# Load buffers moved to multiples of 512 bytes, two more of them, 4096-byte rows for the experts' second layers, and an earlier place for the overflow branch

## The chip, the cores and the metric

The kernel runs on one core of a Trainium2 chip. The metric is the device time of one execution in microseconds (us); lower is better. The kernel before has a median of 1852.47 us in 3 runs (1851.46 to 1853.66).

## What is computed

Two transformer blocks on 256 tokens of width 1024, all in float32. The first block has a mixer (sparse attention and block attention) and a mixture of 32 experts, of which each token uses 4. The second block puts 16 meta tokens ahead (272 rows) and has a stick-breaking attention layer, an MLP, a gated linear recurrence, a second MLP and a last norm. The part that the change is mostly about is the mixture of experts:

```python
def sparse_moe(h, router_w, router_b, w1, b1, w2, b2):
    logits = (hf @ router_w + router_b).astype(jnp.float32)
    top_val, top_idx = lax.top_k(logits, TOP_K)              # 4 of 32
    gate = jax.nn.softmax(top_val, axis=-1)
    ...
    def expert_block(args):
        e, toks, wts = args
        u = hf[toks] @ w1[e] + b1[e]                          # 1024 -> 2048
        g_, lin = u[:, :D_FF], u[:, D_FF:]
        g_ = jnp.minimum(g_, SWIGLU_LIMIT)
        lin = jnp.clip(lin, -SWIGLU_LIMIT, SWIGLU_LIMIT)
        y = ((lin + 1.0) * g_ * jax.nn.sigmoid(SWIGLU_ALPHA * g_)) @ w2[e] + b2[e]   # 1024 -> 1024
        return y * wts[:, None]
    y = lax.map(expert_block, ...)
    return jax.ops.segment_sum(...)
```

`exp_w1` is 32 x 1024 x 2048 and `exp_w2` 32 x 1024 x 1024 float32, 402.7 MB in all, or 384 transfers of 1 MB (1,048,576 bytes). Every weight is read once.

## The kernel before

**Loads.** The class `Stream` holds a list of load items of up to 1 MB in the order of use. `pump` issues them from the SP queue (L169) into `wraw` tiles of 128 partitions x 2048 floats. A load is issued when the buffer that comes next in the rotation is free. The rotation has a fixed depth, and `widen(places, until)` adds buffers in named places of an arena (`r1`, `s2`, ...) up to an item number. Each DMA counts on one of eight semaphores (`DMAHW0` to `DMAHW7`), which are used in turn, and a load waits until the one before it on its semaphore has landed, so at most eight are in flight. In the dense layers `split_to` turns each raw tile into a high and a low part (ACT copies at L189, DVE or POOL subtracts at L191); the experts use the raw tiles.

**Experts.** The 32 experts are sorted by their number of tokens and worked off in 17 jobs: 15 pairs with 64 slots each and two single ones with 128. `queue_moe` queues w1 of job i (8 items for each expert, 128 rows of 8192 bytes), then w2 of job i-1 (4 items for each expert). The 16 w1 items of the first job are known before the routing (`known`); all later ones are addressed by the routing result. A w2 item is 256 rows of 1024 floats, laid out so that partition p has rows 2p and 2p+1, one run of 8192 bytes. `moe` runs, for i from 0 to 17, `mm1` of job i (PE, L1442, and the bias, L1444), then its activation `act_steps` (DVE L1468, L1465, L1472, L1475 and ACT L1469 on the tile `gl`, which sits in arena place s5, and the transposes `turn`, PE L1501 and ACT L1502, and `slots`), then `mm2` of job i-1 (PE L1535, evictions on ACT L1543 and DVE L1544, and the sum back into the tokens, PE L1558 and L1559, DVE L1563). The `turn` steps of job i are run between the matmuls of `mm2` of job i-1. The last items are therefore w1 of the last job (353 to 368), w2 of the last but one (369 to 376) and w2 of the last (377 to 384).

**Gather.** Ahead of each group of jobs `gather` picks the tokens' rows with a 0/1 matrix `S`: four fp32r matmuls for a tile of 128 rows (L1407: two token halves x a high part `h2h` and a low part `h2l`), and one DVE instruction (L1409).

**Overfull experts.** An expert with more tokens than its slots leaves the rest to `overflow`: all engines read a count (L1230) and branch on it (`tc.If`, L1231); the body loops over the experts. With this input the count is zero and the body is jumped over. The body's first two loads for each expert go into the tile `ovb`, in arena place s5. `moe` calls it at i = n = 17, after the last activation steps are queued and before `mm2` of the last job:

```python
                    first, second = self.act_steps(self.jobs[i], ctxs[i])
                    self.bg += first
...
                if i >= 1:
                    if i == n:
                        self.overflow()
                        self.st.cut = "DP"
                    out = self.mm2(self.jobs[i - 1], ctxs.pop(i - 1))
```

**Norms of the second block.** `norm_in` squares and adds eight tiles; in its part 1 POOL squares the even ones (L1638), ACT the odd ones (L1640), and POOL and DVE add (L1647), beside DVE's `hn_lo` (L1628).

Of the kernel before, what the change touches and what calls it, by code (L numbers as in the profile page):

```python
# [20 lines left out]
S = 256  # L21
# [196 lines left out]
def _v(pattern, **kw):  # L218
    return lambda t: t.rearrange(pattern, **kw)
# [23 lines left out]
class Ker:  # L243
# [86 lines left out]
    def setup(self):  # L330
        nc, A = self.nc, self.A
        cp = self.cp = self.pool("const")
        self.cst = cp.tile([128, A["keep"].shape[1]], F32, name="cst")
        self.h = cp.tile([128, 8, NT], F32, name="h")
        self.tmp = self.pool("tmp", 2)
        self.eps = cp.tile([128, 1], F32, name="eps")
        nc.vector.memset(self.eps, EPS)
        nc.scalar.preload_act_table_set(LNEXP)

        def c(name):  # L340
            o, n = self.koff[name]
# [17 lines left out]
    def queue_pre(self):  # L359
# [47 lines left out]
        for c in range(2):  # L407
            cs = slice(c * 512, c * 512 + 512)
            st.add([(lambda t, b=b: t.rearrange("p (k n) -> p k n", k=4)[64 * b:64 * b + 64],
                     wo[256 * b:256 * b + 256, cs].rearrange("(k p) n -> p k n", p=64)) for b in range(2)],  # L410
                   [lambda t, m=m: t.rearrange("p (k n) -> p k n", k=4)[:, :, m * 256:m * 256 + 256] for m in range(2)])
            more(2)
        for c in range(2):
            add_half(st, wo[:, c * 512:c * 512 + 512], 512, 512)
# [81 lines left out]
    def pre(self):  # L496
# [4 lines left out]
        with ExitStack() as ctx:  # L501
# [13 lines left out]
            self.queue_moe()  # L515
            self.queue_post()
            self.widen(("r1", "r2", "r3"), self.early)

# [20 lines left out]
            for k in range(8):  # L539
                self.square_in(k, h[:, k, X], S)  # L540
            self.acc = self.ar("s4", [128, 2, 256], F32, "acc")
            s1, s0 = self.ada(1, pa, "tp"), self.ada(0, self.ps_m, "ot")
# [38 lines left out]
    def mixer(self, H, L):  # L581
# [9 lines left out]
        zs = [self.ar("r0", [128, 8, S], F32, "z")]  # L591
        alibi = self.ar("s6", [128, 8, 384], BF16, "alibi")
        gh = pp.tile([128, 8, 24], F32R, name="gh")
# [69 lines left out]
        kcbd = pp.tile([128, 32], F32, name="kcbd")  # L663
        kr = pp.tile([128, 4, 32], F32, name="kr")
        hd = pp.tile([128, 4, 32], F32, name="hd")

# [58 lines left out]
        for i in range(6):  # L725
            self.dense_t(0, H, L, S, ev_norm(0, i, 6), 2 * (i // 3))
            if i == 1:
                self.st.ahead = 4
        self.fill(len(self.bg))
        heads_rs(0)  # L730

        vv = self.vvt[:, 0:1536].rearrange("p (c n) -> p c n", c=2)
# [171 lines left out]
        for i in range(2):  # L904
            self.dense_v(H, L, lambda c, ps, i=i: nc.scalar.copy(out=vm[:, c, i * 256:i * 256 + 256], in_=ps))
        while state.get("done", -1) < 3:
            self.fill()
# [84 lines left out]
    def route_tile(self, m):  # L992
# [3 lines left out]
        if m == 0:  # L996

            self.ms = self.pp.tile([128, 2, 4], F32, name="ms")
            self.xn = self.ar("s2", [128, 2, 1024], F32, "xn")
# [29 lines left out]
    def route(self):  # L1029
# [19 lines left out]

        self.h2h = self.ar("s3", [128, 2, 1024], F32R, "h2h")  # L1050
        self.h2l = self.ar("s4", [128, 2, 1024], F32R, "h2l")
        xn = self.xn

        def rows(q, c, e):
            o = slice(q * 512, q * 512 + 512)
            r, hi, lo, x = rn[:, 0, c:c + 1], self.h2h[:, c, o], self.h2l[:, c, o], self.nat[c][q]
            if e is nc.scalar:
                e.activation(out=hi, in_=x, func=AF.Copy, scale=r)
            elif e is nc.vector:
                e.scalar_tensor_tensor(out=lo, in0=x, scalar=r, in1=hi.bitcast(F32), op0=ALU.mult, op1=ALU.subtract)  # L1060
            else:
                nc.scalar.activation(out=xn[:, c, o], in_=x, func=AF.Copy, scale=r)
                e.tensor_tensor(out=lo, in0=xn[:, c, o], in1=hi.bitcast(F32), op=ALU.subtract)

        for q in range(2):
            for c in range(2):
                rows(q, c, nc.scalar)

# [10 lines left out]
        for c in range(2):  # L1079
            nc.vector.tensor_scalar(out=sel[:, c], in0=lg[:, c], scalar1=mx[:, c, 3:4], scalar2=None, op0=ALU.is_ge)  # L1080
        rows(0, 0, nc.vector)
        for c in range(2):
            rows(1, c, nc.gpsimd)

# [16 lines left out]
        pick()  # L1101
        rows(0, 1, nc.vector)
        for _ in range(3):
# [47 lines left out]
    def gates(self, pool):  # L1151
# [5 lines left out]
        nc.vector.tensor_tensor(out=g, in0=self.g4, in1=r.unsqueeze(2).to_broadcast([128, 2, 4]), op=ALU.mult)  # L1157
        eg = pool.tile([128, 8, 32], F32, name="geq")
        nc.vector.tensor_tensor(out=eg, in0=self.eq, in1=g.rearrange("p c j -> p (c j)").unsqueeze(2).to_broadcast([128, 8, 32]),
# [65 lines left out]
    def overflow(self):  # L1225
# [5 lines left out]
        with tc.If(n > 0):  # L1231
            ep, pm = self.ep, self.pm

            h2 = self.ar("s2", [128, 8, S], F32, "h2")
            xr = self.ar("s1", [128, 2, 1024], F32, "ovr")
            nc.vector.tensor_tensor(out=xr, in0=self.h2h.bitcast(F32), in1=self.h2l.bitcast(F32), op=ALU.add)
            for k in range(8):
# [9 lines left out]
            with tc.For_i(0, N_EXP, 1) as e:  # L1247
# [4 lines left out]
                nc.sync.dma_start(out=bb, in_=A["exp_b1"][0, bass.ds(e, 1), :].rearrange("a (m p) -> p (a m)", p=128))  # L1252
                act = self.ar("s6", [128, 8, S], F32, "ova")
                for m in range(8):
# [36 lines left out]
    def queue_moe(self):  # L1291
# [26 lines left out]
        def add_w2(ps):  # L1318
            for k in range(4):
                for p in ps:  # L1320

                    st.add([(lambda t: t, lambda p=p, k=k: A["exp_w2"][0, expert(p), k * 256:k * 256 + 256, :]
                             .rearrange("a (p k) n -> p (a k n)", k=2))], ["raw"])

# [9 lines left out]
    def moe(self):  # L1334
        nc, tc = self.nc, self.tc
        with ExitStack() as ctx:
# [10 lines left out]
            for i in range(n + 1):  # L1347
                if i < n:
# [29 lines left out]
    def gather(self, gi):  # L1378
# [8 lines left out]
        if gi:  # L1387
            sel = self.ep.tile([128, 2, 256], F32R, name="S", tag="S")
        else:
            sel = self.ar("sg", [128, 2, 128], F32R, "S0")  # L1390
        xs = self.xs[gi] = self.ar(f"s{1 + gi % 2}", [128, 8, 256], F32, "xs")
# [9 lines left out]
        def tile(k):  # L1401
            def go():
                g = self.gather_bank()[:, 0:tot]
                ks = slice(k * 128, k * 128 + 128)
                for i, x in enumerate((self.h2h, self.h2l)):
                    for c in range(2):
                        nc.tensor.matmul(g, lhsT=x[:, c, ks], rhs=sel[:, c, 0:tot], start=(i == c == 0), stop=(i == c == 1))  # L1407

# [43 lines left out]
    def act_steps(self, job, c):  # L1452
# [40 lines left out]
        def turn(q):  # L1493
            def go():
# [4 lines left out]
                for k in range(4):  # L1499
                    kk = q * 4 + k  # L1500
                    nc.tensor.transpose(t[:, k * 128:k * 128 + 128], l.rearrange("s (q p k) -> s q k p", p=128, k=2)[:, kk // 2, kk % 2], self.c("ident"))  # L1501
                nc.scalar.copy(out=c["at"][:, q * 4:q * 4 + 4], in_=t.rearrange("p (k s) -> p k s", k=4))  # L1502
# [107 lines left out]
    def norm_in(self, name, j, n, by_token=False):  # L1610
# [10 lines left out]
        def norm(k, src, part=None):  # L1621
# [13 lines left out]
            else:  # L1635
                sq = self.pc.tile([128, NT], F32, name="sq", tag="nsq", bufs=2)[:, :n]
            if part == 1 and k % 2 == 0:
                nc.gpsimd.tensor_tensor(out=sq, in0=src, in1=src, op=ALU.mult)  # L1638
            else:
                nc.scalar.activation(out=sq, in_=src, func=AF.Square)  # L1640
            if part == 1:

                if k < 2:
                    sums.append(sq)
                else:
                    e = nc.vector if k % 2 else nc.gpsimd
                    e.tensor_tensor(out=sums[k % 2], in0=sums[k % 2], in1=sq, op=ALU.add)  # L1647
                acc = sums[0]
# [612 lines left out]
```

## Time and profile before

| what | value |
|---|---|
| median of 3 runs | 1852.47 us (1851.46 to 1853.66) |
| profiled execution | 1854.01 us, span 1851.9 us, mean granted TensorE clock 0.979 |
| PE busy | 1724.2 us (93%) |
| DVE, ACT, POOL busy | 718.1, 525.4, 270.6 us |
| SP's DMA queue | 546.02 MB, 77.0% of 16 engines' span |
| DMA in the middle of the expert stage | about 421 GB/s, share 1.01 |

The span runs from the first to the last instruction of the profiled execution; what it is short of the execution's time lies around it. A busy share is a mean over stages: the first 95 us or so fetch the modulation weights, the mixer runs to about 237 us, the experts from there to about 1197 us, and the second block from there to the end.

### The profile page before, as it was taken

To read this page: it belongs to the slowest core of one execution; us is meant where nothing else is said; L and a number is where in the kernel's file an instruction comes from. 1 tells how busy PE (TensorE), PEld (TensorE's weight loads), DVE (VectorE), ACT (ScalarE), POOL (GpSimd) and SP (SyncE) were. 2 spreads that over 40 slices of the span, in tenths; PEclk is the share of its full clock that TensorE was granted. 3 is DMA by queue.
4 is the path that set the end of the run, shared out by engine and by line. 5 is a ranking of instruction groups with operands and counts; after the bars stand their busy time and mean duration, and the time that the engine had idled before them with its cause. 6 is when DMAs were issued, how large, how long until landed. Compare 5 with 4: busy or idle time off the path is not lost. (4 is left out here: it accounts for less than half of the span.)

```text
span 1851.9 us, 25047 instructions
## 1 busy us (share of the span) xinstructions
PE 1724.2 (93%) x9964; PEld 1084.6 (59%) x9964; DVE 718.1 (39%) x1252; ACT 525.4 (28%) x953; POOL 270.6 (15%) x231
## 2 busy tenths in 40 slices
PE   6898989998999999998899989799999999989998
PEld 3776743332334333343443333388889999879986
DVE  3455631322222222221222212355575534876622
ACT  4443320000000000000000000246665544856633
POOL 0000020000000000000000000174433343004442
PEclk7999989999999999999999999999999999999999
DMA  9923889999999999999999999852246555446551
GB/s 344 344 73 114 271 335 398 421 420 422 421 422 421 421 422 420 421 421 421 421 422 420 422 421 421 339 179 81 80 137 180 176 169 173 136 128 182 188 192 72
DMA packets 166952, 549.63 MB, mean 297 GB/s; under 512 B 8656, under 2 KB 101840, under 8 KB 117488
## 3 DMA queue, kind: packets, MB, share of 16 engines
q1 hardware_dynamic: 166208, 546.02, 77.0%
q0 software_dynamic: 432, 1.57, 0.3%
q8 instruction: 80, 1.31, 0.3%
q10 hardware_dynamic: 192, 0.40, 0.1%
q14 instruction: 40, 0.33, 0.0%
HBM read 546.91 MB, written 1.05 MB: 296 GB/s over the span
## 5 line engine op out<-in xcount | busy, mean ns | idle before, releaser
L191 POOL TENSOR_TENSOR wsp<-wraw,wsp 128x1024 fp32r<-128x1024 f32 x91 | 220.0, 2420 | 442.7 <-ACT wsp L189 417.8
L1442 PE MATMUL u<-wraw_s,xs 128*64 128x512 f32 (+1 forms) x848 | 248.6, 600 | 7.3 <-DMA wraw_s<-in_exp_w 7.2
L289 PE MATMUL dps<-hn_hi,wsp 128*128 128x272 f32 (+1 forms) x816 | 239.8, 294 | 7.9 <-DVE gt L2120 3.6
L189 ACT CAST wsp<-wraw 128x1024 fp32r<-128x1024 f32 x210 | 217.1, 1042 | 101.3 <-PE f L2175 46.9
L290 PE MATMUL dps<-hn_lo,wsp 128*128 128x272 f32 (+1 forms) x816 | 235.6, 289 | 4.6 <-DVE hn_lo L1628 4.4
L291 PE MATMUL dps<-hn_hi,wsp 128*128 128x272 f32 (+1 forms) x816 | 235.4, 288 | 0.2 <-DVE wsp L191 0.2
L191 DVE TENSOR_TENSOR wsp<-wraw,wsp 128x1024 fp32r<-128x1024 f32 x119 | 150.9, 1275 | 131.8 <-ACT wsp L189 131.6
L1442 PE MATMUL u<-wraw,xs 128*64 128x512 f32 (+1 forms) x600 | 178.9, 613 | 2.0 <-DMA wraw<-in_exp_w 1.9
L1442 PE MATMUL u<-wraw_r,xs 128*64 128x512 f32 (+1 forms) x600 | 178.5, 602 | 1.4 <-DMA wraw_r<-in_exp_w 1.3
L289 PEld LDWEIGHTS dps<-hn_hi,wsp 128*128 128x128 f32 x816 | 155.9, 191 | 13.3 <-issue 4.9
L290 PEld LDWEIGHTS dps<-hn_lo,wsp 128*128 128x128 f32 x816 | 155.8, 191 | 6.6 <-DVE hn_lo L1628 5.9
L291 PEld LDWEIGHTS dps<-hn_hi,wsp 128*128 128x128 f32 x816 | 155.9, 191 | 0.5 <-DVE wsp L191 0.5
L1442 PEld LDWEIGHTS u<-wraw_s,xs 128*64 128x64 f32 (+1 forms) x848 | 72.1, 140 | 120.7 <-issue 98.6
L1563 DVE SCALAR_TENSOR_TENSOR h<-cb,vec,h 128x256 f32<-128x256 f32 x136 | 59.3, 479 | 178.8 <-PE cb L1559 178.8
L1469 ACT ACTIVATE sg<-gl 128x1024 f32<-128x1024 f32 x17 | 18.0, 1057 | 386.1 <-DVE gl L1468 386.1
L1418 POOL CAST pk<-P 128x128 fp32r<-128x128 f32 x17 | 5.3, 311 | 813.4 <-PE u L1444 810.4
L1535 PE MATMUL y<-wraw,at 128*64 128x512 f32 (+1 forms) x360 | 112.6, 606 | 10.7 <-DMA wraw<-in_exp_w 10.7
L1535 PE MATMUL y<-wraw_s,at 128*64 128x512 f32 (+1 forms) x336 | 108.4, 597 | 11.5 <-DMA wraw_s<-in_exp_w 8.0
L1535 PE MATMUL y<-wraw_r,at 128*64 128x512 f32 x328 | 103.9, 596 | 13.4 <-DMA wraw_r<-in_exp_w 13.4
L1544 DVE SCALAR_TENSOR_TENSOR y<-y,gs 128x1024 fp32r<-128x1024 f32 (+1 forms) x18 | 22.0, 1224 | 215.2 <-ACT y L1543 203.4
L1409 DVE TENSOR_SCALAR xs<-gp,a,vec 128x256 f32<-128x256 f32 (+1 forms) x72 | 37.9, 527 | 164.4 <-PE gp L1407 164.3
L1543 ACT ACTIVATE y<-y,gs 128x1024 fp32r<-128x1024 f32 (+1 forms) x18 | 19.2, 1067 | 245.5 <-PE y L1535 245.5
(499 smaller groups left out, 2903.4 us busy)
## 6 DMA issues: line engine op xcount, KB each, us to landing
wraw_s<-in_exp_w SPq DMA_DIRECT2D x148, 1024.0 KB, 19.8
wraw<-in_exp_w SPq DMA_DIRECT2D x120, 1024.0 KB, 19.8
wraw_r<-in_exp_w SPq DMA_DIRECT2D x116, 1024.0 KB, 19.8
wraw<-in_mlp_w_up SPq DMA_DIRECT2D x32, 1024.0 KB, 5.5
wraw<-in_mlp_w_down SPq DMA_DIRECT2D x32, 1024.0 KB, 4.9
wraw<-in_ada_w SPq DMA_DIRECT2D x14, 1024.0 KB, 5.5
wraw<-in_sb_w_qkv SPq DMA_DIRECT2D x12, 1024.0 KB, 5.5
wraw_r<-in_ada_w SPq DMA_DIRECT2D x10, 1024.0 KB, 11.9
```

What stands on the lines that cost most here:

```text
L189: nc.scalar.copy(out=hv, in_=src)
L191: e.tensor_tensor(out=lv, in0=src, in1=lr, op=ALU.subtract)
L289: mm(o, lhsT=wh, rhs=xh, start=first, stop=False)
L290: mm(o, lhsT=wh, rhs=xl, start=False, stop=False)
L291: mm(o, lhsT=wl, rhs=xh, start=False, stop=last)
L1409: nc.vector.tensor_scalar(out=xs[:, k, 0:tot], in0=g, scalar1=self.a2[:, k:k + 1], scalar2=self.mod[:, 24 + k:25 + k], op0=ALU.mult, op1=A ...
L1442: mm(u[n][js], lhsT=xs[:, k, o + j * C:o + j * C + C], rhs=w[:, ns], start=(k == 0), stop=(k == 7))
L1469: nc.scalar.activation(out=sg, in_=g, func=AF.Sigmoid, scale=1.702)
L1535: mm(y[n][js], lhsT=at[:, k, js], rhs=w[:, cs], start=(k == 0), stop=(k == 7))
L1543: nc.scalar.activation(out=yh[:, a], in_=x, func=AF.Copy, scale=gs)
L1544: nc.vector.scalar_tensor_tensor(out=yl[:, a], in0=x, scalar=gs, in1=yh[:, a].bitcast(F32), op0=ALU.mult, op1=ALU.subtract)
L1563: nc.vector.scalar_tensor_tensor(out=h[:, m, META:NT], in0=o, scalar=self.mod[:, 40 + m:41 + m], in1=h[:, m, META:NT], op0=ALU.mult, op1=A ...
```

## The change

The edits are: the tile `eps`, which is allocated ahead of the load buffers, grows from 1 to 104 columns, so that the load buffers (`wraw`, `wsp` and the arena) move from 128 bytes past a multiple of 512 to a multiple of 512 in each partition. Two more arena places serve as load buffers: s4 until the mixer's last part is queued (`late`), and s3 from the end of the mixer to the second block (`post_first`), which takes the steady rotation of the expert stage from 13 to 14 buffers, and lets all 16 known items be loaded ahead. The places come free because the gather now reads one float32 tile `h2` with two matmuls instead of `h2h` and `h2l` with four. The w2 items are laid out as two rows of 4096 bytes in each partition, and `turn` reads its source without the stride. `overflow` is called at i = n-1, after `mm1` of the last job and before its `act_steps`. `norm_in` no longer uses POOL in part 1. `st.ahead = 4` is set a little later.

```diff
-        self.eps = cp.tile([128, 1], F32, name="eps")
+        self.eps = cp.tile([128, 104], F32, name="eps")[:, 0:1]
...
+            self.widen(("s4",), self.late)
             self.widen(("r1", "r2", "r3"), self.early)
...
+        self.widen(("s3",), self.post_first)
...
-        self.h2h = self.ar("s3", [128, 2, 1024], F32R, "h2h")
-        self.h2l = self.ar("s4", [128, 2, 1024], F32R, "h2l")
...
+            if c:
+                nc.vector.tensor_scalar(out=self.h2[:, c, o], in0=x, scalar1=r, scalar2=None, op0=ALU.mult)
             else:
...
+                nc.scalar.activation(out=self.h2[:, c, o], in_=x, func=AF.Copy, scale=r)
...
-                act = self.ar("s6", [128, 8, S], F32, "ova")
+                act = self.ar("s0", [128, 8, S], F32, "ova")
...
-                    st.add([(lambda t: t, lambda p=p, k=k: A["exp_w2"][0, expert(p), k * 256:k * 256 + 256, :]
-                             .rearrange("a (p k) n -> p (a k n)", k=2))], ["raw"])
+                    st.add([(_v("p (k n) -> p k n", k=2), lambda p=p, k=k: A["exp_w2"][0, expert(p), k * 256:k * 256 + 256, :]
+                             .rearrange("a (k p) n -> p (a k) n", p=128))], ["raw"])
...
                     self.mm1(self.jobs[i], c, tiles, early)
                     self.fill(len(self.bg))
+                    if i == n - 1:
+                        self.overflow()
                     first, second = self.act_steps(self.jobs[i], ctxs[i])
...
                     if i == n:
-                        self.overflow()
                         self.st.cut = "DP"
...
-                for i, x in enumerate((self.h2h, self.h2l)):
-                    for c in range(2):
-                        nc.tensor.matmul(g, lhsT=x[:, c, ks], rhs=sel[:, c, 0:tot], start=(i == c == 0), stop=(i == c == 1))
+                for c in range(2):
+                    nc.tensor.matmul(g, lhsT=self.h2[:, c, ks], rhs=sel[:, c, 0:tot], start=(c == 0), stop=(c == 1))
...
-            if part == 1 and k % 2 == 0:
-                nc.gpsimd.tensor_tensor(out=sq, in0=src, in1=src, op=ALU.mult)
-            else:
-                nc.scalar.activation(out=sq, in_=src, func=AF.Square)
+            nc.scalar.activation(out=sq, in_=src, func=AF.Square)
...
-                    e = nc.vector if k % 2 else nc.gpsimd
-                    e.tensor_tensor(out=sums[k % 2], in0=sums[k % 2], in1=sq, op=ALU.add)
+                    nc.vector.tensor_tensor(out=sums[k % 2], in0=sums[k % 2], in1=sq, op=ALU.add)
```

**SP at the end of the experts.** Before, SP stands at the end of the branch after all 384 expert loads, and the loads of the second block follow (`in_sb_w_qkv`):

```order
L1276 DMA ovw_6690<-in_exp_w 128x8x128 [waits DMAHW1_49,PE_49]
L1247 REGISTER_ALU
L1247 COMPARE_AND_BRANCH
L1231 UNCONDITIONAL_BRANCH [waits DMAHW0_49,DMAHW1_49,DMAHW2_49,DMAHW3_49,DMAHW4_49,DMAHW5_49,DMAHW6_49,DMAHW7_49]
L169 DMA wraw<-in_sb_w_qkv 128x8x256 [waits DMAHW4_49,DMAHW3_49,PE_49]
L169 DMA wraw<-in_sb_w_qkv 128x8x256 [waits DMAHW5_49,DMAHW4_49,PE_49]
```

In the changed kernel the last two expert loads (items 383 and 384) stand behind it:

```order
L1241 REGISTER_ALU
L1241 COMPARE_AND_BRANCH
L1226 UNCONDITIONAL_BRANCH [waits DMAHW0_49,DMAHW1_49,DMAHW2_49,DMAHW3_49,DMAHW4_49,DMAHW5_49,DMAHW6_49,DMAHW7_49]
L169 DMA wraw<-in_exp_w 128x2x1024 [waits DMAHW1_49,PE_49]
L169 DMA wraw<-in_exp_w 128x2x1024 [waits DMAHW2_49,PE_49]
L169 DMA wraw<-in_sb_w_qkv 128x8x256 [waits DMAHW3_49,PE_49]
L169 DMA wraw<-in_sb_w_qkv 128x8x256 [waits DMAHW5_49,DMAHW4_49,PE_49]
```

The row with the eight waits is the end of the path that is taken when no expert is overfull: SP waits for each semaphore and then adds to it what the body's loads would have added.

**DVE at the last job's activation.** Before, the four instructions on `gl` come ahead of the branch, and the row after the branch is a sum into the tokens:

```order
L1468 TENSOR_SCALAR gl<-u 128x1024 [waits PE_49]
L1465 TENSOR_SCALAR gl<-u 128x1024 [waits PE_49]
L1472 SCALAR_TENSOR_TENSOR gl<-gl 128x1024 [waits DVE_49]
L1475 TENSOR_TENSOR gl<-gl,sg 128x1024 [waits DVE_49,Activation_49]
L1486 TENSOR_SCALAR st<-sb,cst 128x256 [waits PE_49]
...
L1544 SCALAR_TENSOR_TENSOR y<-y,gs 128x1024 [waits Activation_49]
L1230 TENSOR_LOAD nov [waits DVE_49]
L1231 COMPARE_AND_BRANCH
```

In the changed kernel they follow the branch, and the first of them waits for two of the load semaphores:

```order
L1226 UNCONDITIONAL_BRANCH [waits DVE_49]
L1461 TENSOR_SCALAR gl<-u 128x1024 [waits DMAHW0_49,DMAHW7_49,DVE_49,PE_49]
L1458 TENSOR_SCALAR gl<-u 128x1024 [waits PE_49]
L1465 SCALAR_TENSOR_TENSOR gl<-gl 128x1024 [waits DVE_49]
L1468 TENSOR_TENSOR gl<-gl,sg 128x1024 [waits DVE_49,Activation_49]
L1479 TENSOR_SCALAR st<-sb,cst 128x256 [waits PE_49]
```

The two semaphores are those of the two loads into `ovb` in the branch's body, which share place s5 with `gl`; in the built program the values waited for are 896 and 880, and SP's straight path brings them from 880 and 864 to 944 and 928, as its first and its eighth step.

**PE at the same place.** In the changed kernel PE goes on behind the branch with `mm2` of the last job but one, and the first transpose of `gl` (L1494) stands between its matmuls:

```order
L1226 UNCONDITIONAL_BRANCH [waits PE_49]
L1528 MATMUL y<-wraw,at 64x512 [waits DMAHW0_49,DVE_49]
L1528 MATMUL y<-wraw,at 64x512 [waits DMAHW1_49]
...
L1476 MATMUL sb<-SG,pe 128x512 [waits PE_49,DVE_49,Activation_49,Pool_49]
...
L1494 MATMUL at_ps<-cst,gl 128x128 [waits DVE_49,PE_49]
```

In the kernel before the same row has the name L1501 and the branch stands after the last matmul of that `mm2`.

## Rows read from the trace of the kernel before

**Rows 1.** The page: span, and DMA in 40 slices of it.

```profile
span 1851.9 us, 25047 instructions
...
DMA  9923889999999999999999999852246555446551
GB/s 344 344 73 114 271 335 398 421 420 422 421 422 421 421 422 420 421 421 421 421 422 420 422 421 421 339 179 81 80 137 180 176 169 173 136 128 182 188 192 72
```

**Rows 2.** Stretches: length; busy PE, PEld, DVE, ACT, POOL; PEclk; DMA share; GB/s.

```profile
400.00:750.00 350.00, 333.60 (x1412) 129.03 (x1410) 82.94 (x141) 21.23 (x26) 3.81 (x14) 1.00 1.01 421
750.00:1100.00 350.00, 331.55 (x1416) 128.42 (x1414) 84.39 (x137) 21.11 (x25) 3.21 (x12) 1.00 1.01 421
```

**Rows 3.** DMA, 400 to 1100 us: packets, bytes; queue: packets, MB, share.

```profile
DMA packets 40451, 294.81 MB, mean 421 GB/s; under 512 B 4489, under 2 KB 4489, under 8 KB 4489
...
q1 hardware_dynamic: 40417, 294.34, 101.1%
```

**Rows 4.** DMA view of 9 to 17 us, loads of the modulation weights.

```profile
DMA packets 875, 3.28 MB, mean 410 GB/s; under 512 B 59, under 2 KB 80, under 8 KB 875
...
q1 hardware_dynamic: 875, 3.28, 101.8%
```

**Rows 5.** Busy time by stretch at the start of the expert stage.

```profile
241.00:258.00 17.00, 12.89 (x47) 7.02 (x47) 8.48 (x31) 4.43 (x10) 4.87 (x10) 0.53 0.96 395
258.00:299.00 41.00, 40.26 (x190) 15.61 (x190) 11.73 (x23) 2.61 (x4) 0.53 (x2) 1.00 0.91 346
299.00:320.00 21.00, 21.00 (x93) 7.23 (x91) 1.96 (x4) 1.17 (x2) 0.54 (x2) 1.00 1.01 424
```

**Rows 6.** Waits of SP's queue from 235 to 300 us.

```profile
SPq L169 <- PE u L1442: 43.3, 8, 15.4
```

**Rows 7.** Timeline of PE at 251 us, and a float32 matmul of 256 columns (L703).

```profile
251.31 6.45 PE L1442 MATMUL u<-wraw,xs 128*64 128x512 f32 x16
257.69 0.51 PE L1407 MATMUL gp<-S,h2h 128*128 128x256 f32 x2
258.03 0.40 PE L1407 MATMUL gp<-S,h2l 128*128 128x256 f32 x2
...
L703 PE MATMUL hs<-sq,once x28: 377/379/483, 50.5 to 158.3; 128*128 128x256 f32 x28
```

**Rows 8.** SP around the branch: timeline, and line L1231.

```profile
1162.57 7.79 SPq L169 DMA_DIRECT2D wraw<-in_exp_w  x4
1191.28 5.41 SPq L169 DMA_DIRECT2D wraw<-in_sb_w_qkv  x4
...
L1231 SPq EVENT_SEMAPHORE  x8: 17/17/17, 1176.1 to 1191.1; - x8
```

**Rows 9.** Timeline of DVE at the last job's activation.

```profile
1152.03 1.23 DVE L1468 TENSOR_SCALAR gl<-u 128x1024 f32<-128x1024 f32 x1 [9.00 <-PE u L1442]
...
1156.33 1.23 DVE L1475 TENSOR_TENSOR gl<-gl,sg 128x1024 f32<-128x1024 f32 x1
```

**Rows 10.** Timeline of PE from the last job's transposes to its end.

```profile
1166.84 0.74 PE L1501 MATMUL at_ps<-cst,gl 128*128 128x128 f32 x4
...
1173.12 0.59 PE L1535 MATMUL y<-wraw_s,at 128*64 128x512 f32 x1
1177.21 1.94 PE L1535 MATMUL y<-wraw_s,at 128*64 128x512 f32 x8 [3.50 <-PEq L1231]
...
1187.34 7.46 PE L1535 MATMUL y<-wraw,at 128*64 128x512 f32 x32
```

**Rows 11.** Behind the experts: DVE's timeline, PE's waits, busy time by stretch.

```profile
1199.37 8.84 DVE L1628 SCALAR_TENSOR_TENSOR hn_lo<-h,vec,hn_hi 128x272 fp32r<-128x272 f32 x8
...
PE dps L290 <- DVE hn_lo L1628: 2.6, 2, 1.6
...
1203.00:1209.00 6.00, 5.76 (x25) 5.77 (x26) 6.00 (x8) 3.29 (x5) 5.76 (x8) 0.50 0.88 278
1209.00:1220.00 11.00, 10.25 (x77) 9.72 (x76) 7.48 (x12) 3.54 (x5) 5.80 (x14) 0.99 0.86 262
```

More of the change, by code (lines that the diff above doesn't have):

```diff
@@ L412, in queue_pre @@
             more(2)
+        self.late = len(st.items)
         for c in range(2):
@@ L540, in pre @@
                 self.square_in(k, h[:, k, X], S)
-            self.acc = self.ar("s4", [128, 2, 256], F32, "acc")
+            both = self.ar("s6", [128, 2048], F32, "both")
+            self.alibi = both[:, 0:1536].bitcast(BF16).rearrange("p (j n) -> p j n", j=8)
+            self.acc = both[:, 1536:2048].rearrange("p (i n) -> p i n", i=2)
             s1, s0 = self.ada(1, pa, "tp"), self.ada(0, self.ps_m, "ot")
@@ L591, in mixer @@
         zs = [self.ar("r0", [128, 8, S], F32, "z")]
-        alibi = self.ar("s6", [128, 8, 384], BF16, "alibi")
+        alibi = self.alibi
         gh = pp.tile([128, 8, 24], F32R, name="gh")
@@ L663, in mixer @@
         kcbd = pp.tile([128, 32], F32, name="kcbd")
-        kr = pp.tile([128, 4, 32], F32, name="kr")
-        hd = pp.tile([128, 4, 32], F32, name="hd")
+        kr, hd = (self.vvt[:, o:o + 128].rearrange("p (j n) -> p j n", j=4) for o in (1024, 640))
         def ckeys():
@@ L726, in mixer @@
             self.dense_t(0, H, L, S, ev_norm(0, i, 6), 2 * (i // 3))
-            if i == 1:
-                self.st.ahead = 4
         self.fill(len(self.bg))
         heads_rs(0)
+        self.st.ahead = 4
         vv = self.vvt[:, 0:1536].rearrange("p (c n) -> p c n", c=2)
@@ L998, in route_tile @@
             self.ms = self.pp.tile([128, 2, 4], F32, name="ms")
-            self.xn = self.ar("s2", [128, 2, 1024], F32, "xn")
+            self.xn = self.h2 = self.ar("s4", [128, 2, 1024], F32, "h2")
             self.lt = self.ps_m.tile([128, 512], F32, name="lt", tag="ss", bufs=1)
@@ L1048, in route, with rows @@
         self.tap("lg", lg)
-        self.h2h = self.ar("s3", [128, 2, 1024], F32R, "h2h")
-        self.h2l = self.ar("s4", [128, 2, 1024], F32R, "h2l")
-        xn = self.xn
-        def rows(q, c, e):
+        def rows(q, c):
             o = slice(q * 512, q * 512 + 512)
[L1056 to L1060, printed above, removed]
-            else:
-                nc.scalar.activation(out=xn[:, c, o], in_=x, func=AF.Copy, scale=r)
-                e.tensor_tensor(out=lo, in0=xn[:, c, o], in1=hi.bitcast(F32), op=ALU.subtract)
-        for q in range(2):
-            for c in range(2):
-                rows(q, c, nc.scalar)
+            r, x = rn[:, 0, c:c + 1], self.nat[c][q]
+            if c:
+                nc.vector.tensor_scalar(out=self.h2[:, c, o], in0=x, scalar1=r, scalar2=None, op0=ALU.mult)
+            else:
+                nc.scalar.activation(out=self.h2[:, c, o], in_=x, func=AF.Copy, scale=r)
+        rows(0, 0)
+        rows(1, 0)
         mx = pp.tile([128, 2, 8], F32, name="mx")
@@ L1080, in route @@
             nc.vector.tensor_scalar(out=sel[:, c], in0=lg[:, c], scalar1=mx[:, c, 3:4], scalar2=None, op0=ALU.is_ge)
-        rows(0, 0, nc.vector)
-        for c in range(2):
-            rows(1, c, nc.gpsimd)
+        rows(0, 1)
         rk = self.ps_m.tile([128, 512], F32, name="rk", tag="ss", bufs=1)
@@ L1101, in route @@
         pick()
-        rows(0, 1, nc.vector)
+        rows(1, 1)
         for _ in range(3):
@@ L1157, in gates @@
         nc.vector.tensor_tensor(out=g, in0=self.g4, in1=r.unsqueeze(2).to_broadcast([128, 2, 4]), op=ALU.mult)
-        eg = pool.tile([128, 8, 32], F32, name="geq")
+        eg = pool.tile([128, S], F32, name="gj", tag="gj").rearrange("p (j e) -> p j e", j=8)
         nc.vector.tensor_tensor(out=eg, in0=self.eq, in1=g.rearrange("p c j -> p (c j)").unsqueeze(2).to_broadcast([128, 8, 32]),
@@ L1234, in overflow @@
             h2 = self.ar("s2", [128, 8, S], F32, "h2")
-            xr = self.ar("s1", [128, 2, 1024], F32, "ovr")
-            nc.vector.tensor_tensor(out=xr, in0=self.h2h.bitcast(F32), in1=self.h2l.bitcast(F32), op=ALU.add)
+            xr = self.h2
             for k in range(8):
@@ L1387, in gather @@
         if gi:
-            sel = self.ep.tile([128, 2, 256], F32R, name="S", tag="S")
+            sel = self.ep.tile([128, 2, 256], F32, name="S", tag="S")
         else:
-            sel = self.ar("sg", [128, 2, 128], F32R, "S0")
+            sel = self.ar("sg", [128, 2, 128], F32, "S0")
         xs = self.xs[gi] = self.ar(f"s{1 + gi % 2}", [128, 8, 256], F32, "xs")
@@ L1404, in go @@
                 ks = slice(k * 128, k * 128 + 128)
-                for i, x in enumerate((self.h2h, self.h2l)):
-                    for c in range(2):
-                        nc.tensor.matmul(g, lhsT=x[:, c, ks], rhs=sel[:, c, 0:tot], start=(i == c == 0), stop=(i == c == 1))
+                for c in range(2):
+                    nc.tensor.matmul(g, lhsT=self.h2[:, c, ks], rhs=sel[:, c, 0:tot], start=(c == 0), stop=(c == 1))
                 nc.vector.tensor_scalar(out=xs[:, k, 0:tot], in0=g, scalar1=self.a2[:, k:k + 1],
@@ L1500, in go @@
                     kk = q * 4 + k
-                    nc.tensor.transpose(t[:, k * 128:k * 128 + 128], l.rearrange("s (q p k) -> s q k p", p=128, k=2)[:, kk // 2, kk % 2], self.c("ident"))
+                    nc.tensor.transpose(t[:, k * 128:k * 128 + 128], l[:, kk * 128:kk * 128 + 128], self.c("ident"))
                 nc.scalar.copy(out=c["at"][:, q * 4:q * 4 + 4], in_=t.rearrange("p (k s) -> p k s", k=4))
```

## The prediction, made before the changed kernel ran

> **What bounds the kernel now.** I read the span in slices first [rows 1]: from slice 8 to slice 25 DMA stands at 9 tenths and some 421 GB/s, and before and behind that at far less. So for some 850 of 1852 us, the expert stage, the loads set the pace. The view by stretch bears this out [rows 2]: DMA's share is 1.01 in both stretches, while PE's matmuls take 665 of 700 us in half-filled tiles that overlap, with waits for loads in between. In this stage a transfer that takes longer costs its full excess, and PE work in a job costs nothing as long as it stays short of the loads. One transfer of 1 MB takes 1.0486 MB / 421 GB/s = 2.491 us [rows 2].
>
> At the start the loads are not yet the bound: from 258 to 299 us PE is busy for 40.26 of 41 us and DMA's share is 0.91; from 299 us on it is 1.01 [rows 5]. SP stands 43.3 us in 8 waits for `mm1` to give buffers back [rows 6].
>
> At the end, what counts is the last landing. SP sees the last of its eight semaphores complete at 1191.1 us [rows 8], and PE's last matmuls end at 1187.34 + 7.46 = 1194.8 us [rows 10], 3.7 us behind it. PE stood 3.50 us at the branch, at 1173.7 us, and this cost nothing, since it would have waited for the last loads all the same. The second block follows only when the experts are summed, so whatever moves 1194.8 moves the end.
>
> **4096-byte rows.** The packets of the middle stretch are 40417 - 4489 = 35928 rows of 8192 bytes [rows 3]. At 421 GB/s over 16 engines one takes 8192 / 26.3 = 311 ns. The trace has 4096-byte rows at saturation too, those of the modulation weights: 410 GB/s at a share of 101.8%, with 80 packets of 875 under 2 KB [rows 4], or 4096 / 25.6 = 160 ns. Two of these are 9 ns more than one of 8192 bytes, so a row costs about 8.3 ns fixed and the rest by its bytes. A w2 transfer goes from 2.491 to 1.0486 / 0.410 = 2.558 us, and there are 128: **+8.6 us**. Bounds: +8.6 if the rate is that of rows 4, and 0 if the few short packets explain the difference.
>
> **Multiples of 512.** No view shows what the offset of a destination does, since all load buffers sit at one offset now. Bounds: nothing at all, or the whole fixed part of a row. The whole is 8 rows x 8.3 ns = 0.066 us for each transfer as it is now: over some 368 transfers that stand in the bound stage 24 us, and about 3 us on the loads of the first 95 us. That would also take back the +8.6. I take **0**: the fixed part of rows of 4096 and 8192 bytes comes out alike for each row, as an overhead of a descriptor would, and nothing in the trace ties it to the offset.
>
> [...]
>
> **Two more buffers.** In the expert stage the lead grows by one transfer, at most **-2.5 us**, as the stretch with a share of 0.91 shows that the queue has idle time to give [rows 5]; the low bound of the gain is 0, if PE's `mm1` (40.26 of 41 us) sets the pace until 299 us anyway. I take -1.5. The s4 buffer of the mixer adds to a stage whose DMA slices stand at 2 and 3 [rows 1]; it waits for nothing, 0.
>
> **Gather.** Four fp32r matmuls of a tile of 256 columns run from 257.69 to 258.43 us, 0.74 us [rows 7]. Two float32 matmuls of the same shape at 379 ns each [rows 7] give 0.76. In later jobs both hide behind the loads, and if that cover were gone the 0.02 would count for the 8 tiles of a group, 0.2 us. **0**.
>
> **The branch.** This is the large term. The straight path of SP is not free: its eight semaphore steps stretch from 1176.1 to 1191.1 us [rows 8], because each waits until the last load on its semaphore has landed. Before, nothing but the second block's loads stood behind it (1191.28 [rows 8]). In the changed kernel items 383 and 384 stand behind it, and on DVE the last job's activation: the first instruction on `gl` waits for two of the semaphores, one of which SP raises in its eighth step. SP takes that step when item 382 has landed, two transfers ahead of the last: 1191.1 - 2 x 2.49 = 1186.1 us on the old time axis. Before, the activation began at 1152.03 and ended at 1156.33 + 1.23 = 1157.56 [rows 9].
>
> So: activation from 1186.2, 5.5 us, to 1191.7. PE has long been at the first transpose, which it reached at 1166.84 before [rows 10]; behind that in its queue stand the rest of `mm2` of the last job but one and all of `mm2` of the last. What it still has to do from there: 1166.84 to 1173.71 (6.9 us), about 1.2 us until ACT has moved the first half of y out, and 1177.21 to 1194.80 (17.6 us) [rows 10]. 1191.7 + 0.1 + 6.9 + 1.2 + 17.6 = 1217.5, against 1194.8: +22.7. Items 383 and 384, issued at 1186 into an empty queue, land by about 1194 and are not needed before 1210.
>
> PE stands still for 25 us in this. [...] From 1203 to 1209 us the granted clock was 0.50 after a few light microseconds, too [rows 11]. The bounds are 0 and 2.7, and I take 2.5. **+25 us** in all. The cover that would hide it does not exist: the second block's loads start some 5 us earlier, but the first of its matmuls wait for the norm of the sum.
>
> **Norms.** `hn_lo` takes 8.84 us for 8 beside POOL's squares [rows 11], but PE waits only 2.6 us for it [rows 11], and ACT gets four squares more. Between 0 and -2.6: **-1 us**.
>
> **Sum.** Against the profiled execution's 1854.0: +8.6 + 0 - 1.5 + 25 - 1 = 1885.1; it lay 1.5 above the median of the runs, so **1884 us** (A).
>
> **The rivals.**
> B, the start at a multiple of 512 takes away half of the fixed part. For: the part exists in every row [rows 3, 4]. Against: it looks like a cost of a row, not of a place. w1's 240 transfers in the bound stage gain 0.033 us each, 8 us; w2 in 16 rows with 4.15 ns costs what 8 rows with 8.3 ns did, so the +8.6 is gone; the first stage gains 1.5. 1884 - 8.6 - 8 - 1.5 = **1866 us**.
> C, it takes away all of it: 1884 - 8.6 - 24 - 3 = **1848 us**, which is faster. From 2.425 us for a transfer downwards (a rate of 432 GB/s and up) the loads give back more than the branch costs; above that they do not. For: nothing but the bound. Against: the highest slices of the expert stage show 422 [rows 1].
> D, DVE's wait costs little, because the semaphore values are there when it looks, or PE finds other work: only a stop like the 3.50 us at the branch now [rows 10] is added, and 1884 - 25 + 3.5 = **1862 us**. Against: the values waited for are raised by SP alone, and SP's steps in the trace keep pace with the landings [rows 8].
> E, the branch costs more: SP itself reaches the branch later, and items 383 and 384 hold PE up as well, 2 x 2.5 us more, 1889 us.
>
> **How the numbers follow.** A 0.55 (1875 to 1887), B 0.2, D 0.1, C 0.08, E 0.07. The range has to hold 8 in 10 and takes in A, B, D and E, and leaves out C: 1859 to 1891 us. The bounds of A's own small terms (-8.6 for the rows, -1 to +1.5 for the buffers, -2.5 for the clock, -1.6 to +1 for the norm) lie inside it. A measurement of this kernel can tell about 0.2% from no change. Faster than that is the better half of C (0.04) and B together with D (0.04): 0.08. Within 0.2% (1848.8 to 1856.2): the rest of C and the edge of B, 0.05. Slower: 0.87.
>
> **What the profile would show.** SP's semaphore steps of the branch end ahead of the last two expert loads; DVE stands some 30 us ahead of its first `gl` of the last job; PE stands some 25 us at L1494, and the first half of what follows may run at half clock; 1 MB w2 loads land 2.56 us apart (A) or 2.49 (B) or less (C); w1 loads 2.49 (A), 2.46 (B) or 2.425 (C), read as 421, 426 or 432 GB/s in a stretch with w1 alone. I would be wrong if DVE's first `gl` ran near 1153, or if the expert stage ran above 428 GB/s as a whole.

## The result: 1.0% slower, and the profile after

The changed kernel has a median of 1871.9 us in 4 runs (1870.28 to 1873.34), against 1853.07 us for the kernel before (4 runs, one more than when its profile was taken): the ratio is 1.0100, with an interval of 1.0083 to 1.0118, so some 19 us slower. The prediction said 1884 us, in a range of 1859 to 1891.

The lines of the changed kernel's page that answer to [rows 1]:

```profile
span 1868.4 us, 25027 instructions
...
DMA  9923699999999999999999999462236545446552
GB/s 348 353 75 106 203 361 380 426 424 424 424 425 423 426 426 423 424 425 424 423 426 426 424 424 422 190 227 89 62 125 186 181 162 177 136 136 181 183 192 76
```

In the expert stage the loads run at 424 instead of 421 GB/s, although a third of the bytes now comes in 4096-byte rows. At the end of the stage two slices fall to 190 and 227. Three places differ: the branch and the mixer cost time, and the loads give some back.

**The branch.** The timelines of SP, DVE and PE at the last job and SP's steps at the branch, answering to [rows 8 to 10]. Columns of a timeline: start, length, engine, line, operation, tiles, count, and in brackets the idle time ahead of it with what ended it.

```profile
1166.80 20.11 SPq L169 DMA_DIRECT2D wraw<-in_exp_w  x3
1187.02 27.30 SPq L169 DMA_DIRECT2D wraw<-in_sb_w_qkv  x2
...
L1226 SPq EVENT_SEMAPHORE  x8: 17/17/17, 1174.3 to 1185.6; - x8
...
L1226 SPq COMPARE_BRANCH  x1: 50/50/50, 1169.3 to 1169.3; - x1
...
1185.78 1.22 DVE L1461 TENSOR_SCALAR gl<-u 128x1024 f32<-128x1024 f32 x1 [42.79 <-SPq L1226]
...
1189.49 1.23 DVE L1468 TENSOR_TENSOR gl<-gl,sg 128x1024 f32<-128x1024 f32 x1
...
1190.87 1.09 PE L1494 MATMUL at_ps<-cst,gl 128*128 128x128 f32 x4 [22.73 <-DVE gl L1468]
1191.88 3.46 PE L1528 MATMUL y<-wraw_r,at 128*64 128x512 f32 x8
1195.27 0.66 PE L1494 MATMUL at_ps<-cst,gl 128*128 128x128 f32 x4
...
1213.73 3.60 PE L1528 MATMUL y<-wraw,at 128*64 128x512 f32 x16
```

DVE stood 42.79 us, until SP's eighth semaphore step at 1185.6 us let it go at 1185.78. PE stood 22.73 us at the first transpose, and the eight matmuls behind it took 3.46 us, where [rows 10] have 1.94 for eight: the granted clock was 0.50 from 1191 to 1195 us and 1.00 from 1195 to 1200 (columns as in [rows 2]).

```profile
1191.00:1195.00 4.00, 4.00 (x12) 1.32 (x12) 0.54 (x3) 0.58 (x1) 0.00 (x0) 0.50 1.05 396
1195.00:1200.00 5.00, 5.00 (x26) 1.91 (x26) 0.00 (x0) 0.97 (x2) 0.00 (x0) 1.00 0.12 40
```

**The mixer.** It ends late: the first matmuls of the routing (tile `lt`) start at 231.6 us instead of 222.4, and the first of the experts at 259.7 instead of 251.31 [rows 7]. The `lt` rows, of the kernel before and then of the changed one:

```profile
222.38 0.53 PE L1009 MATMUL lt<-rwa,h 128*128 128x32 f32 x4
...
231.64 0.53 PE L1013 MATMUL lt<-rwa,h 128*128 128x32 f32 x4
```

Waits (columns: total, times, longest) of SP (95 to 235 us) and ACT (150 to 235), in the kernel before:

```profile
SPq L169 <- PE adap L436: 37.0, 8, 7.9
...
ACT wsp L189 <- DMA wraw<-in_w_out: 3.3, 2, 2.9
```

The same in the changed kernel, and PE's longest wait (150 to 262):

```profile
SPq L169 <- PE adap L438: 46.0, 6, 16.1
...
ACT wsp L189 <- DMA wraw<-in_w_out: 12.1, 2, 6.4
ACT wsp L189 <- DMA wraw_s<-in_w_out: 3.0, 1, 3.0
...
PE ot L862 <- ACT ap L852: 4.3, 1, 4.3
```

One load of the modulation weights waited 16.1 us for its buffer (7.9 at most before) and was issued at 176.81 us, and two loads of w_out, which stand behind it in SP's order, from 177.82 us on; ACT's splits of w_out waited 15.1 us for them (3.3 before), and in ACT's queue behind the splits stood the copies that the attention needs. PE waited 4.3 us for such a copy, which it did not before.

**The loads.** The DMA view of 400 to 1100 us of the changed kernel, answering to [rows 3]:

```profile
DMA packets 52723, 297.15 MB, mean 424 GB/s; under 512 B 4527, under 2 KB 4527, under 8 KB 28424
...
q1 hardware_dynamic: 52687, 296.66, 101.4%
```

They made up for the late mixer: by the trace's landing records item 382, the third last load of the experts, landed at 1185.5 us, against 1186.2 before.

### The profile page after: what moved, and what is told of

It is laid out like the page before. It is cut to its first block, busy times and chain, and to the rows that moved or that the text cites. A ratio compares the mean times of both kernels' runs of the same rounds, so it can differ in the third digit from the quotient of the medians.

```text
span 1868.4 us, 25027 instructions
## 1 busy us (share of the span) xinstructions
PE 1738.2 (93%) x9964; PEld 1089.2 (58%) x9964; DVE 712.0 (38%) x1255; ACT 524.3 (28%) x953; POOL 262.3 (14%) x222
## 5 line engine op out<-in xcount | busy, mean ns | idle before, releaser
L1435 PE MATMUL u<-wraw_s,xs 128*64 128x512 f32 (+1 forms) x888 | 287.2, 600 | 0.5 <-DMA wraw_s<-in_exp_w 0.5
L1435 PE MATMUL u<-wraw,xs 128*64 128x512 f32 (+1 forms) x600 | 218.6, 607 | 5.0 <-DMA wraw<-in_exp_w 5.0
L191 DVE TENSOR_TENSOR wsp<-wraw,wsp 128x1024 fp32r<-128x1024 f32 x117 | 147.1, 1263 | 136.3 <-ACT wsp L189 136.2
L1435 PE MATMUL u<-wraw_r,xs 128*64 128x512 f32 (+1 forms) x560 | 151.5, 603 | 1.2 <-DMA wraw_r<-in_exp_w 1.2
L1435 PEld LDWEIGHTS u<-wraw_s,xs 128*64 128x64 f32 (+1 forms) x888 | 80.4, 140 | 123.5 <-issue 117.1
L1528 PE MATMUL y<-wraw_s,at 128*64 128x512 f32 (+1 forms) x432 | 135.3, 596 | 4.0 <-DMA wraw_s<-in_exp_w 4.0
L1528 PE MATMUL y<-wraw,at 128*64 128x512 f32 (+1 forms) x288 | 99.1, 608 | 8.6 <-DMA wraw<-in_exp_w 5.4
L1435 PEld LDWEIGHTS u<-wraw,xs 128*64 128x64 f32 (+1 forms) x600 | 59.6, 141 | 64.5 <-issue 50.5
L1528 PEld LDWEIGHTS y<-wraw_s,at 128*64 128x64 f32 (+1 forms) x432 | 43.7, 141 | 77.6 <-issue 67.6
```

The costliest lines, as they stand in the source:

```text
L191: e.tensor_tensor(out=lv, in0=src, in1=lr, op=ALU.subtract)
L1435: mm(u[n][js], lhsT=xs[:, k, o + j * C:o + j * C + C], rhs=w[:, ns], start=(k == 0), stop=(k == 7))
L1528: mm(y[n][js], lhsT=at[:, k, js], rhs=w[:, cs], start=(k == 0), stop=(k == 7))
```

## The experiments

Each run has its own ratio to the kernel before, from runs on the same chip; these ratios are compared, as the kernel before itself came out between 1850 and 1857 us. One percent is 18.5 us.

| run | edit | median us | ratio (interval) |
|---|---|---|---|
| changed kernel | | 1871.9 | 1.0100 (1.0083 to 1.0118) |
| 1 | changed, `gl` of the last job in s4 | 1853.45 | 1.0001 (0.9991 to 1.0011) |
| 2 | changed, branch back | 1851.6 | 0.9991 (0.9981 to 1.0000) |
| 3 | changed, no s4 in the mixer | 1866.49 | 1.0075 (1.0058 to 1.0092) |
| 4 | changed, buffers at 128 past | 1891.9 | 1.0211 (1.0194 to 1.0228) |
| 5 | changed, buffers at 256 past | 1872.23 | 1.0101 (1.0084 to 1.0118) |
| 6 | changed, buffers at 32 past 256 | 1897.81 | 1.0245 (1.0228 to 1.0262) |
| 7 | before, 4096-byte rows alone | 1864.19 | 1.0061 (1.0044 to 1.0078) |
| 8 | run 2 without s4 in the mixer | 1845.5 | 0.9957 (0.9944 to 0.9970) |
| 9 | run 8 with 8192-byte rows | 1839.84 | 0.9936 (0.9911 to 0.9961) |
| 10 | run 9 with `ahead` early | 1836.7 | 0.9915 (0.9893 to 0.9937) |
| 11 | run 2 with POOL in the norm | 1851.99 | 0.9996 (0.9986 to 1.0007) |
| 12 | before, buffers at multiples of 512 alone | 1837.29 | 0.9901 (0.9883 to 0.9919) |

### Runs 1 and 2: which part of the branch costs

The theory was that DVE's wait at `gl` costs the time; the rival, that SP's drain and the two loads behind it would do so without it. Run 1 takes away what makes DVE wait, by another place for the tile:

```diff
-        gl = self.ar("s5", [128, 2, 1024], F32, "gl")
+        gl = self.ar("s4" if job is self.jobs[-1] else "s5", [128, 2, 1024], F32, "gl")
```

> The changed kernel, but the last job's gl sits in arena place s4 instead of s5, so that DVE's first instruction behind the branch no longer waits for the load semaphores; SP's drain of the eight loads and the place of items 383 and 384 stay. If the wait at gl is the cost (my theory): PE follows the last landing (1193.4 us) by about 4 us as in the kernel before, the experts end near 1198 instead of 1218 us, and the time falls by about 20 us to 1852 us (1848 to 1856). If the drain and the two loads behind it hold PE up by themselves (rival): above 1865 us.

Run 2 moves the call back (and the body's `ova` to s6, as before):

```diff
-                    if i == n - 1:
-                        self.overflow()
...
                     if i == n:
+                        self.overflow()
```

> The changed kernel with the branch back at its old place, ahead of the last job's second layer. My theory: the activation begins near 1152 us again, the last load lands near 1191 us and the experts end near 1195 us, so the time falls by 22 to 24 us, to 1849 us (1846 to 1853). If the place of the branch is not what costs (rival), it stays above 1865 us. Against the run with gl in another place it says what the drain alone costs: some 3 us by theory.

Measured: 1853.45 and 1851.6 us, that is 1.0% and 1.1% below the changed kernel, both as the theory had it. In the timeline of run 1 the activation starts at 1158.05, released by PE's own step at the branch, while SP's order is as in the changed kernel:

```profile
1158.05 1.23 DVE L1461 TENSOR_SCALAR gl<-u 128x1024 f32<-128x1024 f32 x1 [13.60 <-PEq L1226]
...
1195.40 3.65 PE L1528 MATMUL y<-wraw,at 128*64 128x512 f32 x14 [1.44 <-DMA wraw<-in_exp_w]
...
1168.08 20.66 SPq L169 DMA_DIRECT2D wraw<-in_exp_w  x3
1188.85 26.28 SPq L169 DMA_DIRECT2D wraw<-in_sb_w_qkv  x6
```

So of the 20 us that the moved branch costs, about 18 are DVE's wait at `gl`. That leaves 2 (1853.45 - 1851.6) for the drain, that is, for SP's steps and the two loads behind them; the intervals overlap, so this part is not shown.

### Runs 3 and 8: the extra buffer in the mixer

```diff
-            self.widen(("s4",), self.late)
```

> The changed kernel without the extra buffer s4 in the mixer's rotation. My theory: the extra buffer shifts the rotation, so that w_out's loads wait in SP's queue behind a modulation load whose buffer is freed late, and the mixer ends 9 us later than in the kernel before (first routing matmul at 231.6 instead of 222.4 us). Without it the first routing matmul is back near 222 to 224 us, and as the expert stage is bound by loads and the known loads can start earlier, most of the 9 us come back: 1864 us (1861 to 1867). Rival: the known loads hide the mixer's delay, and only 0 to 2 us come back: 1870 to 1872 us.

> The changed kernel with the branch at its old place and without the buffer s4 in the mixer. If the two costs are apart and add up: 1851.6 - 5.4 = 1846 us (1844 to 1849). If the loads have the slack to hide one of them: 1850 to 1852 us.

Run 3 gave 1866.49 us, 0.25% less than the changed kernel, the better part of what was expected; run 8, the same edit with the branch back, 0.34% less than run 2. The intervals overlap a little in the first pair and are apart in the second, so the rival, that the known loads hide all of the mixer's delay, is out. The waits of run 3, in the windows used above:

```profile
SPq L169 <- PE adap L438: 43.2, 7, 11.4
...
ACT wsp L189 <- DMA wraw<-in_w_out: 3.7, 2, 2.9
```

ACT's wait for w_out is down from 15.1 to 3.7 us and PE's 4.3 us for ACT's copy are gone. The first `lt` is at 228.8 us, 2.8 earlier than in the changed kernel but 6.4 later than before, so s4 is not the only thing that delays the mixer; run 10 finds most of the rest.

### Runs 4 to 6: the offset of the load buffers

Run 4 gives `eps` one column again, run 5 40 columns and run 6 48; in the built programs the `wraw` buffers start at 128, 256 and 288 bytes past a multiple of 512.

```diff
-        self.eps = cp.tile([128, 104], F32, name="eps")[:, 0:1]
+        self.eps = cp.tile([128, 1], F32, name="eps")
```

> The changed kernel with eps back at one column, so that the load buffers start 128 bytes past a multiple of 512 again; nothing else. If the offset does nothing (what I had taken in the prediction), the rate from 400 to 1100 us stays at 424 GB/s and the time at 1872 us. If the offset is what lifted the rate (now the likelier one, since the rate rose from 421 to 424 GB/s although a third of the bytes went to 4096-byte rows), it falls to the 417 GB/s that 421 for w1 and 410 for w2 give, and the time rises by 850 x 7/424 = 14 us to 1886 us.

> The changed kernel with eps at 40 columns: the load buffers start at 256 past a multiple of 512, which is a multiple of 256. [...] If it takes a multiple of 512, or if another offset is as bad as 128, the rate is 417 GB/s and the time 1892 us, as at 128 bytes past.

> The changed kernel with eps at 48 columns, so that the load buffers start 32 bytes past a multiple of 256. [...] If any start off a multiple of 256 costs the same (an extra access for each row, whatever its length): 1892 us and 417 GB/s.

Measured against the changed kernel: +1.1% for run 4 (20 us, where 14 were expected), nothing for run 5, +1.45% for run 6. The DMA views of 400 to 1100 us, run 4, 5 and 6:

```profile
DMA packets 51362, 292.10 MB, mean 417 GB/s; under 512 B 4447, under 2 KB 4447, under 8 KB 27012
```

```profile
DMA packets 52664, 297.12 MB, mean 424 GB/s; under 512 B 4528, under 2 KB 4528, under 8 KB 28310
```

```profile
DMA packets 51472, 291.31 MB, mean 416 GB/s; under 512 B 4435, under 2 KB 4435, under 8 KB 27437
```

The offset counts, and a multiple of 256 is enough (run 5, 424 GB/s). A start 32 bytes past a multiple of 256 costs the loads of the expert stage no less than one 128 past (416 and 417 GB/s), so the cost does not go by the bytes below the start. The rate does not hold all of the loss: the mixer ends later as well, its first `lt` at 235.4 us in run 4 and 239.9 in run 6, against 231.6. That goes some way to explain the 6 us that run 4 lies above its expectation and the 6 us by which run 6 exceeds run 4; no run has the mixer's share by itself.

### Runs 7 and 9: rows of 4096 bytes at either offset

Run 7 gives the kernel before the new w2 rows and the `turn` that goes with them; run 9 undoes both in run 8.

```diff
-                    st.add([(lambda t: t, lambda p=p, k=k: A["exp_w2"][0, expert(p), k * 256:k * 256 + 256, :]
-                             .rearrange("a (p k) n -> p (a k n)", k=2))], ["raw"])
+                    st.add([(_v("p (k n) -> p k n", k=2), lambda p=p, k=k: A["exp_w2"][0, expert(p), k * 256:k * 256 + 256, :]
+                             .rearrange("a (k p) n -> p (a k) n", p=128))], ["raw"])
```

> The kernel before with the 4096-byte rows for w2 alone, buffers at the old offset. By the prediction's term 1853.1 + 8.6 = 1862 us, and 417 GB/s from 400 to 1100 us. Rival, that 4096-byte rows cost more at this offset than the modulation loads showed, since they suffer from the offset twice as often: 1866 us or more. If short packets explained the difference: 1853 us.

> As the run without s4 and with the branch back, but with w2 in rows of 8192 bytes as in the kernel before, at the new offset. If a row has a fixed cost at this offset too (8192-byte rows at 309 ns, 4096-byte rows at 159 ns, so 9 ns for each pair, 8 pairs in a transfer and 128 transfers): 9 us less, 1837 us, and 428 to 430 GB/s from 400 to 1100 us. If the offset takes the fixed cost away (rival C's mechanism): no change, 1846 us and 424 GB/s.

Run 7: +0.6%, 11 us (8 to 14 by its interval). Run 9: -0.2% against run 8 (0.9936 and 0.9957), 4 to 6 us, between its two expectations; the intervals overlap, and the rates, 427 against 424 GB/s, speak for a gain. The DMA views of 400 to 1100 us, run 7 and then run 9:

```profile
DMA packets 51736, 291.99 MB, mean 417 GB/s; under 512 B 4450, under 2 KB 4450, under 8 KB 27783
...
q1 hardware_dynamic: 51703, 291.54, 101.5%
```

```profile
DMA packets 40978, 298.64 MB, mean 427 GB/s; under 512 B 4548, under 2 KB 4548, under 8 KB 4548
...
q1 hardware_dynamic: 40942, 298.16, 100.9%
```

From these, 700 us x 16 engines over the rows (each with its share of the 4-byte packets): an 8192-byte row takes 11,200 us / 35,928 = 311.7 ns at the old offset [rows 3] and 11,200 us / (40942 - 4548) = 307.7 at the new one. In run 7 there are 51736 - 27783 - 33 (other queues) = 23,920 rows of 8192 bytes and 27783 - 4450 = 23,333 of 4096; a short one takes (11,200 us - 23,920 x 311.7 ns) / 23,333 = 160.5 ns. In the changed kernel, with 24,263 and 23,897 rows by the same count, it takes (11,200 us - 24,263 x 307.7 ns) / 23,897 = 156.3 ns. Two short rows thus cost an estimated 9.3 ns more than a long one at the old offset and 4.9 at the new one, and a row of either length costs some 4 ns less at the new offset.

### Runs 10 to 12: the rest, and the offset alone

Run 10 sets `st.ahead = 4` where the kernel before does; run 11 gives POOL its part of the norm back.

> The run with 8192-byte rows, the branch back and no s4 in the mixer (1839.8 us), and besides st.ahead = 4 set as early as in the kernel before, after the second tile. If the later place is what still holds the mixer back (its first routing matmul was at 246.0 instead of 243.2 us for the gather, 2.7 us late): 2 to 4 us less, 1837 us. If not: 1840 us.

> The changed kernel with the branch back (1851.6 us), and POOL's squares and adds of the norm back as in the kernel before. The prediction's term: 1 us more, 1852.6 us, not to be told from no change. By the traces the second block gave back some 5 us in the changed kernel; if POOL's part in the norm is the cause: 1856 to 1857 us.

Run 12 is the kernel before with the load buffers moved; the room comes from the change's own placing of three small tiles:

```diff
+        self.eps = cp.tile([128, 104], F32, name="eps")[:, 0:1]
...
+        kr, hd = (self.vvt[:, o:o + 128].rearrange("p (j n) -> p j n", j=4) for o in (1024, 640))
...
+        eg = pool.tile([128, S], F32, name="gj", tag="gj").rearrange("p (j e) -> p j e", j=8)
```

> The kernel before with the load buffers at multiples of 512 alone (eps at 104 columns; room for it is made by the change's own placing of kr, hd and geq in other tiles); 13 buffers, the old gather, 8192-byte rows, the branch at its old place. If the offset alone makes the gain: 427 instead of 421 GB/s over 890 us gives 12 to 13 us, and some of the mixer's 4 us, 1838 to 1841 us, as the best run (1836.7 us). If the other parts of that run (one more buffer in the expert stage, the gather from one tile) carry a share: 1845 us or more.

Run 10: 0.2% below run 9, with overlapping intervals, inconclusive by its time; its first gather matmul is at 240.2 us against 246.0 in run 9, so the mixer did come forward, and its first `lt`, at 220.3 us, is no longer late. Of the mixer's delay the later `st.ahead` thus holds 5.8 us, more than s4. Run 11: no difference to run 2 that could be told from none, as the prediction's 1 us implied. The 6 us that the second block seemed to give back in the changed kernel (from the last sum into the tokens to the end: 646.4 us, against 652.5 before) are not POOL's; the same code there took 646.2 us in run 9's profile and 651.1 in run 10's, so most of this is a difference between single profiled executions. Run 12: 1837.29 us, 1% below the kernel before, just below the 1838 to 1841 us expected if the offset alone makes the gain. One more buffer in the expert stage, the gather from one tile and the norm without POOL, which run 10 has and run 12 has not, show no gain between them. The DMA view of 400 to 1100 us of run 12, and SP's steps at the branch (L1231 in the kernel before, [rows 8]):

```profile
DMA packets 40978, 298.64 MB, mean 427 GB/s; under 512 B 4548, under 2 KB 4548, under 8 KB 4548
...
L1230 SPq EVENT_SEMAPHORE  x8: 17/17/17, 1160.4 to 1175.2; - x8
```

## Why the prediction was right, and where its terms were off

The sign, the range and the mechanism of the large term came out as predicted. Two terms of the sum did not, and a third cost was not in it at all; that they cancelled in part is luck. The measured 1872 us lies below A's own 1875 to 1887, in the part of the range that was there for rival B.

- **The branch, +25.** Right in its place and its chain: activation forecast for 1186.2, seen at 1185.78; PE at L1494 for some 25 us, seen 22.73; a restart at half clock, seen at 0.50; the last `y` matmul forecast to end at 1217.5 us, and at 1220 with the clock, seen at 1217.33. (DVE stood 42.79 us and not some 30, as it reached the branch earlier, which delays nothing.) Measured by run 2: 1.1%, 20 us; the sums into the tokens start 22.1 us later on the time axis (1201.15 against 1179.08), so the term was over-sized by 3 to 5 us. Part of that is the clock, for which 2.5 was taken. The bound of 2.7 is what 16 of the experts' matmuls took at a granted clock of 0.56, from 251.31 us [rows 7], less half of what 32 took at 1.00 [rows 10]; no run shows it for the restart behind the branch, where eight matmuls took 1.5 us more than eight at 1.00 (3.46 against 1.94). Rival D, a branch at 3.5 us, is out, by run 1 as well. E is out: SP reached the branch no later (1169.3 us against 1170.7), and the last two loads landed at 1190.8 and 1193.4, ahead of PE's matmuls on them, from 1210 us on.
- **4096-byte rows, +8.6.** Run 7 gives 11, and 8.6 lies in its interval. At the new offset the term is about half of that, 4 to 6 us (run 9, not clear of noise).
- **Multiples of 512, taken as 0.** This is the step that failed. "Nothing in the trace ties it to the offset" was true, and not evidence against it, as the trace before has one offset only. Run 4 measures 20 us in the changed kernel, run 12 some 17 to 18 in the kernel before. In the expert stage it is a mean of 4 ns for each 8192-byte row, half of the fixed 8.3 that I had worked out: rival B's size, 18 us. In run 12 the last expert load lands at 1175.2 instead of 1191.1 us, of which 2.2 us are ahead of the experts (first `lt` at 220.1 instead of 222.4). The cost does not go by the bytes below the start either: run 6, at 32 bytes past, is 26 us slower than the changed kernel, where a quarter of run 4's 20 us would be 5. The rows of the modulation weights, which gave the 8.3 together with [rows 3], do not show the offset: from 9 to 17 us they run at 410 GB/s in the kernel before and run 4, and at 409 to 412 in the changed kernel and runs 1 to 3.
- **Two more buffers, -1.5.** Failed in the mixer, where I had put s4 at 0, because "it waits for nothing". A buffer more changes which buffer each load gets, and in SP's order of issue one late buffer holds up the loads that follow (16.1 us here). Run 3 and run 8 measure 5 to 6 us for it. In the expert stage no gain shows.
- **`st.ahead` set later.** The sum had no term for it, and gave no reason. By the traces of runs 9 and 10 it delays the mixer by 5.8 us; what that costs in time, some 3 to 4 us, is not clear of noise.
- **Gather 0, norm -1.** No run contradicts them; run 11 shows nothing for the norm, and the gather was not run by itself.

From run 12 to the changed kernel the single edits make a chain: 0.9901, 0.9915 (the buffer s3, gather and norm, run 10), 0.9936 (`ahead` later, run 9), 0.9957 (4096-byte rows, run 8), 0.9991 (s4 in the mixer, run 2), 1.0100 (the branch). The alignment won 1%, the branch lost 1.1%, and the rest lost 0.9% in small steps, of which only that of s4 is clear of noise by itself; the alignment alone would have been a faster kernel.

The mean forecast of 1884 was 12 us high: 20 for the offset and 5 for the branch too high, 5 to 6 for s4, some 4 for `ahead` and 2 for the rows too low, which add up to within 2 us of it. Had s4 and `ahead` cost nothing, the time would by these figures have been some 1862 us, near the low end of the range.

## What to carry to other kernels

A branch like this one is a fence for whatever its body loads, even when it is jumped over: an instruction behind it that reuses such a buffer waits until the loads in flight have landed (18 us here), so put a branch where nothing urgent reuses the body's buffers, or give the body buffers of its own. Where a stage is bound by loads, start the destinations at a multiple of 256 bytes (from 128 past to a multiple of 512 won 1% in run 12, and 256 did as well as 512 in run 5), and keep rows long (4096 instead of 8192 bytes for w2 cost 0.6% in run 7); a trace with one offset can't price another, so leave a wide range for what it does not show. For loads issued in a fixed order, one more buffer is not free by itself (s4 cost 5 to 6 us here): look at which load gets the buffer that is freed last, and at what stands behind it.

## What was not expected of the hardware

In the expert stage destinations 128 bytes past a multiple of 512 cost an estimated mean of 4 ns for each row of 8192 bytes (311.7 against 307.7, from [rows 3] and run 9), 1.4% of the rate (421 against 427 GB/s), and the cost does not shrink when the start is only 32 bytes past (416 GB/s, against 417 at 128 bytes past and 424 at 0 and 256, all with a third of the bytes in 4096-byte rows). It is not the same for each row either: by the packet records of 400 to 1100 us, 99.9% of the 8192-byte rows take 309 ns in the changed kernel, while in the kernel before 26% do and nearly all others spread up to 322. Why a row takes longer is not settled by these runs.
